# Order of the small matrix products of a hybrid diffusion step: alternating array halves, and column groups in whole visits

## The chip, the core and the metric

One core of a Trainium2 chip runs the whole kernel. The metric is the device time of one execution in microseconds, here the median of three runs. TensorE (PE) multiplies, VectorE (DVE), ScalarE (ACT) and GpSimd (POOL) do the elementwise work, and SyncE (SP) issues most of the DMAs. TensorE's array has 128 rows, along which a product sums, and 128 columns, its outputs. A product that needs only 64 rows or only 64 or 32 columns occupies a part of the array.

## The reference, cut

The reference takes 128 context tokens and 512 latent tokens of width 1024 through two layers. In each layer:

```
sh1, sc1, g1, sh2, sc2, g2 = split(silu(c) @ w_mod + b_mod, 6)          # adaLN, per stream
h = rmsnorm(x) * (1 + sc1) + sh1
z, xbc, dt, u, dq, dk, dv, wq, wk, wv = split(h @ w_in)
y_a = ssd_mixer(...)                     # Mamba-2 scan, both directions
y_b = s5_mixer(u, ...)                   # diagonal state space, both directions
y_c: s = q k^T / 8 for two halves (c = 0, 1) of each of 4 heads; softmax each
     (softmax_0 - lam * softmax_1) @ v   # differential attention
y_d: softmax([sink, q k^T / 8 + band mask]) @ v   # 8 query heads, 2 key heads, window 128
x = x + g1 * ((sum of gate_b * (y_b @ w_branch_b)) @ w_out)
x = x + g2 * (relu(rmsnorm(x)... @ w_fc1)^2 @ w_fc2)
```

Queries, keys and window values have 64 numbers a head, so the score products sum over 64 rows, and the window's product with the values has 64 outputs.

## The kernel before, in words

Activations lie feature-major in tiles of 128 features by 640 tokens, worked in halves of 320 tokens. Every large product (`mm3_step`, L221 to L223) is three products of high and low parts, on the whole array, 128 by 128. The weights are loaded by SP, rounded by ACT (L210) into the high part, and DVE or POOL makes the low part (L194).

Four kinds of small products use a part of the array only:

- `adaln` (L277), called by `adaln_ahead` (L304) for 36 pieces of 256 outputs: eight products, k = 0 to 7, each on 32 columns, at column group k mod 4 (L286). Their weights come through the ring `wa`, a quarter of the panel (two k) a DMA. Twelve more pieces, at the start, take theirs from `wm` tiles.
- `s5_build` (L476), eight blocks of four groups in each layer: for each group g, on column group g, four products of 112 columns (L646) and four of 16 (L650, L651), into the bank `pk`.
- `win_core` (L1241): for every token tile t (five) and key head n (two), pairs `hp` of query heads; a score tile `sc` of two banks holds the heads j = 0, 1 of the pair. The score products (L1264, L1266) sum over the 64 rows of key head n; masks are added by products with the identity (L1271); after the softmax and the transposes (L1301) head by head, the products with the values (L1306) write 64 columns, the half n of `po`.
- `diff_core` (L1376): for every token tile t and head h of a call, c = 0 and then c = 1: a score tile `sc` of two banks, filled by two products of 320 keys (L1394; one of 128 for t = 0, L1390) over the 64 rows of half c; then the maxima, the exponentials, the difference, transposes (L1423), the products with the values (L1428) and the square (L1430).

The tiles `sc`, `pt`, `raw` and adaLN's `acc` all come from `mx()`, a ring of two tiles of two PSUM banks.

The order of the work is static. A plan of letters (`PLAN`) advances generators, one step each, so that the chains of several mixers and the large products alternate; a scheduler then orders each engine's instructions ahead of time by priority (the place in the program) as their inputs come ready, and `tc.high_priority(offset=n)` moves what it encloses n places ahead. On the chip each engine takes its instructions in that order. Weights' preparation has `AHEAD = 2000`. In the steps named `b` (S5 matrices of layer 0) and in the MLP of layer 0 (its matrices for layer 1, and adaLN pieces) the small products go between large ones.

Of the kernel before, what the change touches and what calls it, by code (L numbers as in the profile page):

```python
# [39 lines left out]
AHEAD = 2000  # L40
NORM_POOL = (1, 4, 7)
NTAIL = 3
# buffers of the rings of tiles
# [3 lines left out]
# the engine of an elementwise step: v(ector) or p(ool)  # L47
# [4 lines left out]
# of the scan's blocks of latent chunks, those on the vector engine  # L52
SCAN = 5
# every so many low parts of operands is made on the pool engine
# [20 lines left out]
def hybrid_body(ctx: ExitStack, tc: tile.TileContext, a: dict, o: dict, dbg: dict):  # L75
# [21 lines left out]
    # ---------------------------------------------------------------- tiles  # L97
# [6 lines left out]
    def load_const(name, src, shape, into):  # L104
        """A constant, to be loaded behind the first loads, or later."""
        t = const(name, shape)
        into.append((t, src))
        return t
# [92 lines left out]
    def load_w(src, n=512, extra=False, ahead=AHEAD):  # L201
        """(high, low) of a weight tile; extra: in tiles of the phase's pool."""
# [22 lines left out]
    def mm3(ps, terms):  # L225
        """ps = sum over terms of stationary^T moving, each operand a (high, low) pair."""
# [3 lines left out]
    def split_w(w, kk):  # L230
        """Column block kk, of 128, of a panel."""
# [8 lines left out]
    def dense(src, act, evac):  # L240
        """One block of 128 outputs, feature-major: evac(half, psum [128, 320])."""
# [6 lines left out]
    def dense23(srcs, act, evacs):  # L248
        """Two or three blocks of 128 outputs, by halves of the tokens: a function of the half, yielding by block."""
# [12 lines left out]
    def streams(hf):  # L262
        """Token ranges of a half by stream: (stream, first, last) within the half."""
# [4 lines left out]
    # ------------------------------------------------------------- adaLN  # L268
# [8 lines left out]
    def adaln(l, parts, q, acc, out, raw):  # L277
        """mods[l][:, part*8 + 2q + (0, 1), stream] of one or two parts.

        acc: a bank of PSUM; out: 4 columns a part for the results; raw(part, n): quarter n of a panel of weights."""  # L280
        n = len(parts)
        for i, part in enumerate(parts):
            for k in range(KT):
# [4 lines left out]
                    start=(k < 4), stop=(k >= 4),  # L288
# [14 lines left out]
    def adaln_ahead(l, parts, after=()):  # L303
        """The pieces of the given parts, one a step."""  # L304
        for part in parts:
            for q in range(4):
# [9 lines left out]

                acc = mx()
                adaln(l, [part], q, acc[:, 0], acc[:, 1], raw)
# [4 lines left out]
    def step(gen, n=1):  # L323
        """The next n pieces of work that fills gaps."""
# [17 lines left out]
    # ---------------------------------------------------------------- norm  # L342
    def square_into(acc, x, k, hf):
        """acc += x[k]^2 on one half."""
# [8 lines left out]
    def norm_factor(acc, hf):  # L353
        """1/rms by token of one half, a quarter of it in each column; and the last instruction on the tensor engine."""
# [7 lines left out]
    def norm_spread(r, rb, hf):  # L362
        """The factor, on all partitions, into the half's bank of rb; the last instruction on the tensor engine."""
# [7 lines left out]
    def norm_mod(l, which, x, rb, hf, hh, hl):  # L371
        """(high, low) of rmsnorm(x)*g*(1+sc)+sh on one half, feature-major; rb: the norm's factor.

        A block of features a step."""
# [90 lines left out]
    # ------------------------------------------------------- S5 matrices  # L465
    s5m = {}

    def s5_build(l, where, after):
        """Per layer: the chunk matrices of the S5 mixer, into DRAM scratch; in steps, 4 groups each after the first.

        after(): an element of a tile before which no step need begin."""
# [23 lines left out]
        for w, shift in (("c", 0.25), ("s", 0.0)):  # L495
            # turns, less the nearest whole number of them
# [38 lines left out]
        # powers 1..8 of the transition of a chunk: re, -im, im  # L535
# [15 lines left out]
        # coef = (ab - 1) / lambda  # L551
# [19 lines left out]
        # exponents by position: input side, by 7-s (fwd 7-s, bwd s); output side (fwd t+1, bwd 8-t)  # L571
# [670 lines left out]
    def win_core(l, wv, qT, kT, var):  # L1242
# [4 lines left out]
        for t in range(NT):  # L1247
# [10 lines left out]
            for n in range(2):  # L1258
# [51 lines left out]
                if n == 0:  # L1310
                    yield
# [639 lines left out]
```

## Time and profile before

| | |
|---|---|
| median of 3 runs | 3173.34 us (3172.48 to 3176.21) |
| profiled execution | span 3172.2 us |
| PE busy | 3026.8 us, 95% |
| DVE busy | 1754.7 us, 55% |
| ACT busy | 1180.2 us, 37% |
| POOL busy | 956.7 us, 30% |

The profiled execution has no time beside its span; the span stands 1.1 us below the median. Busy is the union of an engine's instructions. A matrix product's record begins when it can enter and ends when its results are written, so that records in a row overlap: what a product costs is the distance of starts, not its duration. The profile's name of a shape, 64\*128 64x320, gives the array's rows and columns in use, and then the moving operand.

### The profile page before, as it was taken

To read this page: it belongs to the slowest core of one execution; us is meant where nothing else is said; L and a number is where in the kernel's file an instruction comes from. 1 tells how busy PE (TensorE), PEld (TensorE's weight loads), DVE (VectorE), ACT (ScalarE), POOL (GpSimd) and SP (SyncE) were. 2 spreads that over 40 slices of the span, in tenths; PEclk is the share of its full clock that TensorE was granted. 3 is DMA by queue.
4 is the path that set the end of the run, shared out by engine and by line. 5 is a ranking of instruction groups with operands and counts; after the bars stand their busy time and mean duration, and the time that the engine had idled before them with its cause. 6 is when DMAs were issued, how large, how long until landed. Compare 5 with 4: busy or idle time off the path is not lost. (4 is left out here: it accounts for less than half of the span.)

```text
span 3172.2 us, 54421 instructions
## 1 busy us (share of the span) xinstructions
PE 3026.8 (95%) x20846; PEld 2777.1 (88%) x20846; DVE 1754.7 (55%) x3866; ACT 1180.2 (37%) x2660; POOL 956.7 (30%) x1058
## 2 busy tenths in 40 slices
PE   8888898999999999999999889989999999999999
PEld 6878888898788889899988879878897899999999
DVE  6978836665532456376235686576674425533333
ACT  4234453243333242323234435423433333422323
POOL 1656505522210322144111670263131113211111
PEclk9999999999899999999999999989998999999999
DMA  7553243224331633444444323522251223222222
GB/s 280 173 171 99 77 134 106 78 94 128 123 98 47 213 114 131 142 145 156 136 147 136 127 78 103 149 86 62 80 188 56 71 90 126 64 75 76 74 77 84
DMA packets 240708, 364.23 MB, mean 115 GB/s; under 512 B 42144, under 2 KB 104352, under 8 KB 240448
## 3 DMA queue, kind: packets, MB, share of 16 engines
q1 hardware_dynamic: 225696, 336.97, 33.4%
q10 hardware_dynamic: 14752, 23.78, 2.1%
q8 instruction: 164, 2.69, 0.3%
q14 instruction: 96, 0.79, 0.1%
HBM read 294.98 MB, written 65.68 MB: 114 GB/s over the span
## 5 line engine op out<-in xcount | busy, mean ns | idle before, releaser
L194 POOL TENSOR_TENSOR wl<-wr,wh 128x512 fp32r<-128x512 f32 x207 | 282.3, 1364 | 1328.0 <-ACT wh L210 1059.2
L210 ACT CAST wh<-wr 128x512 fp32r<-128x512 f32 (+1 forms) x614 | 378.4, 620 | 623.5 <-PE dn L222 557.1
L194 DVE TENSOR_TENSOR wl<-wr,wh 128x512 fp32r<-128x512 f32 (+1 forms) x407 | 318.7, 786 | 326.2 <-ACT wh L210 311.3
L221 PE MATMUL dn<-hh,wh 128*128 128x320 f32 x1328 | 425.2, 320 | 7.2 <-ACT gah L1454 6.5
L223 PE MATMUL dn<-hh,wl 128*128 128x320 f32 x1328 | 423.6, 320 | 6.5 <-DVE wl L194 6.5
L222 PE MATMUL dn<-hl,wh 128*128 128x320 f32 x1328 | 423.2, 319 | 2.9 <-DVE hl L395 2.5
L221 PE MATMUL dn<-fh,wh 128*128 128x320 f32 x1008 | 315.3, 313 | 0.9 <-DVE x L1512 0.8
L221 PE MATMUL dn<-nh,wh 128*128 128x320 f32 x992 | 311.0, 314 | 1.6 <-DVE r L1718 1.6
L222 PE MATMUL dn<-fl,wh 128*128 128x320 f32 x1008 | 312.5, 310 | 0.0
L223 PE MATMUL dn<-fh,wl 128*128 128x320 f32 x1008 | 311.6, 309 | 0.0
L222 PE MATMUL dn<-nl,wh 128*128 128x320 f32 x992 | 308.7, 311 | 2.0 <-DVE nl L395 1.1
L223 PE MATMUL dn<-nh,wl 128*128 128x320 f32 x992 | 307.7, 310 | 0.0
L222 PE MATMUL dn<-wl,hh 128*128 128x256 f32 (+1 forms) x880 | 258.0, 294 | 17.5 <-DVE wl L194 15.0
L221 PEld LDWEIGHTS dn<-hh,wh 128*128 128x128 f32 x1328 | 257.1, 194 | 16.3 <-ACT gah L1454 7.0
L223 PEld LDWEIGHTS dn<-hh,wl 128*128 128x128 f32 x1328 | 256.7, 193 | 14.8 <-issue 7.3
L221 PE MATMUL dn<-wh,hh 128*128 128x256 f32 (+1 forms) x880 | 258.8, 296 | 7.1 <-ACT hsq L1174 3.7
L222 PEld LDWEIGHTS dn<-hl,wh 128*128 128x128 f32 x1328 | 256.9, 194 | 9.8 <-issue 4.5
L223 PE MATMUL dn<-wh,hl 128*128 128x256 f32 (+1 forms) x880 | 256.2, 292 | 0.0
L221 PE MATMUL dn<-B,wh 128*128 128x320 f32 x640 | 207.2, 325 | 9.3 <-ACT B L814 3.3
L1512 DVE SCALAR_TENSOR_TENSOR x<-dn,mod,x 128x192 f32<-128x192 f32 (+2 forms) x240 | 97.9, 436 | 206.3 <-PE dn L223 203.3
L222 PE MATMUL dn<-B,wh 128*128 128x320 f32 x640 | 202.2, 316 | 0.0
L223 PE MATMUL dn<-B,wl 128*128 128x320 f32 x640 | 200.9, 314 | 0.0
(410 smaller groups left out, 7066.1 us busy)
## 6 DMA issues: line engine op xcount, KB each, us to landing
wr<-in_w_fc_dram SPq DMA_DIRECT2D x256, 256.0 KB, 2.6
wa<-in_w_mod_dram SPq DMA_DIRECT2D x144, 256.0 KB, 3.4
wr<-in_w_gate_dram SPq DMA_DIRECT2D x128, 256.0 KB, 2.7
wr<-in_w_tok_dram SPq DMA_DIRECT2D x80, 256.0 KB, 2.9
wr<-in_w_branch_dram SPq DMA_DIRECT2D x64, 256.0 KB, 2.9
acc<-gth SPq DMA_DIRECT2D x48, 320.0 KB, 2.8
gold<-acc SPq DMA_DIRECT2D x48, 320.0 KB, 3.3
wm<-in_w_mod_dram SPq DMA_DIRECT2D x24, 512.0 KB, 8.8
```

Of the source, the lines that this page charges most:

```text
L194: engine.tensor_tensor(out=out, in0=full, in1=hi, op=ALU.subtract)
L210: nc.scalar.copy(out=hi, in_=raw)
L221: nc.tensor.matmul(ps, sh, vh, start=first, stop=False)
L222: nc.tensor.matmul(ps, sh, vl, start=False, stop=False)
L223: nc.tensor.matmul(ps, sl, vh, start=False, stop=last)
L1512: nc.vector.scalar_tensor_tensor(out=xs, in0=ps[:, c0:c1], scalar=mods[l][:, part * 8 + f, s:s + 1], in1=xs, op0=ALU.mult, op1=ALU.add)
```

## The change

- `VISIT = 600`, an offset of priority.
- `adaln` takes the list of its k. `adaln_ahead` asks for the piece's four weight tiles first, and then issues the products in a block of priority VISIT, k from 7 down to 0. The twelve pieces at the start are as before.
- `s5_build`: the loop over the four groups g becomes the innermost one, and the whole is a block of priority VISIT.
- `win_core`: instead of the pairs `hp` of one key head, an iteration takes query head g of both key heads n = 0, 1, bank n of `sc` each, and their score products alternate in n. Where the first key tile and the run behind it are neighbours (t = 1, 2), one product covers both. The masks follow. The products with the values wait for both heads' transposes and alternate in n. Both sets are blocks of priority VISIT.
- `diff_core`: both score tiles are taken at once, and the products alternate, c = 1, 0 for keys b = 0, then for b = 1, in a block of priority VISIT.

All else in the diff is the removal of comments. Its core:

```
+VISIT = 600
-    def adaln(l, parts, q, acc, out, raw):
+    def adaln(l, parts, q, acc, out, raw, ks=range(KT)):
-            for k in range(KT):
+            for n_, k in enumerate(ks):
-                    start=(k < 4), stop=(k >= 4),
+                    start=(n_ < 4), stop=(n_ >= 4),
...
+                for n in range(KT // 2):
+                    raw(part, n)
                 acc = mx()
-                adaln(l, [part], q, acc[:, 0], acc[:, 1], raw)
+                with tc.high_priority(offset=VISIT):
+                    adaln(l, [part], q, acc[:, 0], acc[:, 1], raw, range(KT)[::-1])
...
             pk = pb1()
-            for g in range(4):
-                rows = slice(32 * g, 32 * g + 32)
+            with tc.high_priority(offset=VISIT):
                 for c0, c1, z0, t0 in ((0, 112, 16, 1), (128, 240, 0, 0)):
-                    for ri in range(2):
+                    for ri in (1, 0):
+                        for g in range(4):
+                            nc.tensor.matmul(
+                                pk[32 * g:32 * g + 32, c0:c1], bz[:, ri, g, z0:z0 + 32],
+                                qt[:, ri, g, t0:t0 + 7].rearrange("p t m -> p (t m)"), start=(ri == 1), stop=(ri == 0),
+                            )
+                for ri, cc in ((0, craw[:, 0]), (1, ncr[:, 1])):
+                    for g in range(4):
                         nc.tensor.matmul(
+                            pk[32 * g:32 * g + 32, 112:128], bz[:, ri, g, 48:80], cc[:, g], start=(ri == 0),
+                            stop=(ri == 1),
                         )
...
+            rows = [slice(64 * n, 64 * n + 64) for n in range(2)]
+            whole_run = nk > 1 and run[0] == lone + 1
+            for g in range(4):
+                sc = mx()
+                with tc.high_priority(offset=VISIT):
+                    for k0, k1 in [(lone, run[1])] if whole_run else [(lone, lone + 1)] + [run] * (nk > 1):
+                        c0 = 0 if k0 == lone else 128
+                        for n in range(2):
                             nc.tensor.matmul(
+                                sc[:, n, c0:c0 + (k1 - k0) * 128], qT[rows[n], g, ct],
+                                kT[rows[n], k0:k1].rearrange("p k c -> p (k c)"), start=True,
+                                stop=not masks or k1 == lone + 1,
                             )
...
+                with tc.high_priority(offset=VISIT):
+                    for k in range(nk):
+                        for n in (1, 0):
                             nc.tensor.matmul(
+                                po[rows[n], g * 128:(g + 1) * 128], wv[:, idx[k], rows[n]], pT[n][:, k],
                                 start=(k == 0), stop=(k == nk - 1),
                             )
...
+                nb, w = (1, 128) if nk == 1 else (2, HF)
+                raw = [mx(), mx()]
+                with tc.high_priority(offset=VISIT):
+                    for b in range(nb):
+                        for c in (1, 0):
+                            gr = slice(64 * c, 64 * c + 64)
+                            keys = kT[gr, h, k0:k0 + nk].rearrange("p k c -> p (k c)")
+                            nc.tensor.matmul(
+                                raw[c][:, b, 0:w], qT[gr, h, ct], keys[:, b * w:(b + 1) * w], start=True, stop=True
+                            )
```

## Rows read from the trace of the kernel before

**Rows 1.** The page: busy time by engine, and PE in 40 slices.
```profile
PE 3026.8 (95%) x20846; PEld 2777.1 (88%) x20846; DVE 1754.7 (55%) x3866; ACT 1180.2 (37%) x2660; POOL 956.7 (30%) x1058
PE   8888898999999999999999889989999999999999
```

**Rows 2.** Busy time by stretch: PE, PEld, DVE, ACT, POOL; granted clock; DMA share, GB/s.
```profile
100.00:215.00 115.00, 99.77 (x870) 94.91 (x871) 104.91 (x195) 32.27 (x73) 82.12 (x84) 0.94 0.54 181
250.00:350.00 100.00, 85.29 (x510) 79.98 (x510) 96.81 (x193) 34.15 (x82) 76.64 (x123) 0.90 0.22 71
850.00:1010.00 160.00, 159.94 (x1045) 135.40 (x1044) 60.48 (x142) 59.31 (x143) 25.20 (x24) 1.00 0.26 84
1050.00:1700.00 650.00, 644.29 (x4707) 585.68 (x4705) 318.92 (x736) 198.19 (x408) 162.66 (x151) 1.00 0.45 147
2420.00:2580.00 160.00, 160.00 (x1045) 134.41 (x1044) 65.15 (x141) 58.62 (x143) 25.66 (x24) 1.00 0.23 77
```

**Rows 3.** Groups by line and form: shapes, count, busy us, mean ns, idle before.
```profile
L646 PE MATMUL pb<-s5qt,s5bz 128*32 128x112 f32 x512 | 58.3, 275 | 5.3 <-DVE s5qt L589 3.3 <-DVE s5bz L609 2.0
L286 PE MATMUL mx<-wa,cpad 128*32 128x256 f32 x576 | 63.3, 388 | 0.0
```

**Rows 4.** Timeline of PE at a differential score visit: start, us, line, tiles, shape, count.
```profile
655.31 0.27 PE L1423 MATMUL mx<-ident,dp 128*128 128x128 f32 x1
655.51 1.34 PE L1394 MATMUL mx<-d,BT 64*128 64x320 f32 x4
...
657.01 0.28 PE L223 MATMUL dn<-wh,hl 128*128 128x256 f32 x1
657.12 0.28 PE L221 MATMUL dn<-wh,hh 128*128 128x256 f32 x1
```

**Rows 5.** The same where two halves stand together; first the first two records alone.
```profile
1812.08 0.38 PE L1390 MATMUL mx<-d,dq 64*128 64x128 f32 x2
...
1812.08 0.49 PE L1390 MATMUL mx<-d,dq 64*128 64x128 f32 x4
1812.51 0.39 PE L221 MATMUL dn<-wh,hh 128*128 128x272 f32 x1
```

**Rows 6.** The same in the window attention: two heads' scores, then products with values.
```profile
897.55 0.49 PE L1264 MATMUL mx<-wkT,xs 64*128 64x128 f32 x2
897.87 0.81 PE L1266 MATMUL mx<-wkT,xs 64*128 64x384 f32 x2
898.83 0.48 PE L1264 MATMUL mx<-wkT,xs 64*128 64x128 f32 x2
899.89 1.09 PE L1306 MATMUL pb<-wp,wv 128*64 128x128 f32 x8
```

**Rows 7.** The same at an S5 block: its first products, and the next large ones.
```profile
1367.93 0.95 PE L646 MATMUL pb<-s5qt,s5bz 128*32 128x112 f32 x8
...
1371.17 0.21 PE L651 MATMUL pb<-s5nc,s5bz 128*32 128x16 f32 x2
1371.32 0.42 PE L221 MATMUL dn<-fh,wh 128*128 128x320 f32 x1
```

**Rows 8.** The same at adaLN: a visit of four records, and a whole piece.
```profile
1066.67 0.63 PE L286 MATMUL mx<-wa,cpad 128*32 128x256 f32 x4
1067.23 0.42 PE L221 MATMUL dn<-mh,wh 128*128 128x320 f32 x1
...
1237.25 1.07 PE L286 MATMUL mx<-wa,cpad 128*32 128x256 f32 x16
1238.25 0.42 PE L221 MATMUL dn<-fh,wh 128*128 128x320 f32 x1
```

**Rows 9.** Busy time of L1306 alone by stretch: PE and count, PEld, clock, DMA.
```profile
850.00:1010.00 160.00, 25.23 (x182) 19.19 (x182) 1.00 0.26 84
2420.00:2580.00 160.00, 27.83 (x200) 21.07 (x200) 1.00 0.23 77
```

**Rows 10.** What TensorE's idle time before L1394 ended with.
```profile
  ACT mx L1430: 2.1, 5
```

More of the change, by code (lines that the diff above doesn't have):

```diff
@@ L1257, in win_core @@
             po = pb1()
-            for n in range(2):
-                gr = slice(64 * n, 64 * n + 64)
-                for hp in range(2):
-                    sc = mx()
-                    for j in range(2):
-                        q = qT[gr, 2 * hp + j, ct]
-                        nc.tensor.matmul(sc[:, j, 0:128], q, kT[gr, lone], start=True, stop=True)
-                        if nk > 1:
+            rows = [slice(64 * n, 64 * n + 64) for n in range(2)]
+            whole_run = nk > 1 and run[0] == lone + 1
@@ L1266, in win_core @@
+            for g in range(4):
[4 more added lines that the diff above has]
+                        for n in range(2):
                             nc.tensor.matmul(
-                                sc[:, j, 128:nk * 128], q, kT[gr, run[0]:run[1]].rearrange("p k c -> p (k c)"),
-                                start=True, stop=not masks,
-                            )
@@ L1270, in win_core @@
-                            for i, (pos, mk) in enumerate(masks):
-                                nc.tensor.matmul(
-                                    sc[:, j, (1 + pos) * 128:(2 + pos) * 128], identb, maskb[:, mk],
-                                    start=False, stop=(i == len(masks) - 1),
-                                )
-                    scv = sc[:, :, :nk * 128]
-                    m = tmp([128, 2], "wm")
-                    nc.vector.tensor_reduce(out=m, in_=scv, axis=AX.X, op=ALU.max)
@@ new lines, in win_core @@
+                                sc[:, n, c0:c0 + (k1 - k0) * 128], qT[rows[n], g, ct],
+                                kT[rows[n], k0:k1].rearrange("p k c -> p (k c)"), start=True,
+                                stop=not masks or k1 == lone + 1,
+                            )
+                    for n in range(2):
+                        for i, (pos, mk) in enumerate(masks):
+                            nc.tensor.matmul(
+                                sc[:, n, (1 + pos) * 128:(2 + pos) * 128], identb, maskb[:, mk],
+                                start=False, stop=(i == len(masks) - 1),
+                            )
@@ new lines, in win_core @@
+                scv = sc[:, :, :nk * 128]
+                m = tmp([128, 2], "wm")
+                nc.vector.tensor_reduce(out=m, in_=scv, axis=AX.X, op=ALU.max)
+                sk = sink[:, g::4]
+                nc.vector.scalar_tensor_tensor(out=m, in0=m, scalar=0.125, in1=sk, op0=ALU.mult, op1=ALU.max)
+                nm_ = tmp([128, 2], "wnm")
+                nc.vector.tensor_scalar(out=nm_, in0=m, scalar1=-1.0, scalar2=None, op0=ALU.mult)
+                p = [tw([128, 512], "wp") for _ in range(2)]
@@ new lines, in win_core @@
+                sm = tmp([128, 2], "wsm")
+                for n in range(2):
+                    nc.scalar.activation(
+                        out=p[n][:, :nk * 128], in_=scv[:, n], func=AF.Exp, bias=nm_[:, n:n + 1], scale=0.125,
+                        accum_out=sm[:, n:n + 1],
+                    )
+                es = tmp([128, 2], "wes")
+                nc.vector.tensor_tensor(out=es, in0=sk, in1=m, op=ALU.subtract)
+                nc.scalar.activation(out=es, in_=es, func=AF.Exp)
+                nc.vector.tensor_tensor(out=sm, in0=sm, in1=es, op=ALU.add)
@@ new lines, in win_core @@
+                rc = tmp([128, 2], "wrc")
+                nc.vector.reciprocal(out=rc, in_=sm)
+                pt = mx()
+                pT = []
+                for n in range(2):
+                    pn = p[n][:, :nk * 128]
+                    nc.vector.tensor_scalar(out=pn, in0=pn, scalar1=rc[:, n:n + 1], scalar2=None, op0=ALU.mult)
+                    for k in range(nk):
+                        kc = slice(k * 128, (k + 1) * 128)
+                        nc.tensor.transpose(pt[:, n, kc], p[n][:, kc], ident)
+                    pT.append(pn.rearrange("p (k c) -> p k c", c=128))
+                    nc.scalar.copy(out=pT[n], in_=pt[:, n, :nk * 128].rearrange("p (k c) -> p k c", c=128))
@@ L1308, in win_core @@
+                with tc.high_priority(offset=VISIT):
+                    for k in range(nk):
+                        for n in (1, 0):
+                            nc.tensor.matmul(
+                                po[rows[n], g * 128:(g + 1) * 128], wv[:, idx[k], rows[n]], pT[n][:, k],
                                 start=(k == 0), stop=(k == nk - 1),
                             )
-                if n == 0:
+                if g == 1:
                     yield
@@ L1383, in diff_core @@
                 scs, ms = [], tmp([128, 2], "dm")
-                for c in range(2):
-                    gr = slice(64 * c, 64 * c + 64)
-                    sc = mx()
-                    keys = kT[gr, h, k0:k0 + nk].rearrange("p k c -> p (k c)")
-                    q = qT[gr, h, ct]
-                    if nk == 1:
-                        nc.tensor.matmul(sc[:, 0, 0:128], q, keys, start=True, stop=True)
-                        sv = sc[:, 0:1, 0:128]
-                    else:
-                        for b in range(2):
-                            nc.tensor.matmul(sc[:, b, 0:HF], q, keys[:, b * HF:(b + 1) * HF], start=True, stop=True)
-                        sv = sc[:, :, 0:HF]
+                nb, w = (1, 128) if nk == 1 else (2, HF)
[5 more added lines that the diff above has]
+                            keys = kT[gr, h, k0:k0 + nk].rearrange("p k c -> p (k c)")
+                            nc.tensor.matmul(
+                                raw[c][:, b, 0:w], qT[gr, h, ct], keys[:, b * w:(b + 1) * w], start=True, stop=True
+                            )
+                for c in range(2):
+                    sv = raw[c][:, 0:nb, 0:w]
                     nc.vector.tensor_reduce(out=ms[:, c:c + 1], in_=sv, axis=AX.XY, op=ALU.max)
```

33 lines of the change are left out of this document (removed).

## The prediction

> **What bounds the kernel now.** I read the page first: PE is busy for 3026.8 of 3172.2 us, in no slice under 80%, and no other engine over 55% [rows 1]. That average has two kinds of stretch, so the table by stretch comes second [rows 2]. In the second half of the window attention of either layer (850 to 1010 and 2420 to 2580 us) and in the MLP of layer 0 (1050 to 1700 us) PE is busy 99 to 100% and DVE at most half: there a microsecond off PE is a microsecond off the kernel. In 100 to 215 and 250 to 350 us DVE is busy 91 and 97% and PE 87 and 85%: there DVE's chain sets the end, and the granted clock of 0.94 and 0.90 shows that TensorE spends a part of the time at 1.2 instead of 2.4 GHz, because it waits. The groups by line come third [rows 3]. Every product that the code writes stands in the trace as two records: `s5_build` issues 16 products of 112 columns a block, 16 blocks, and L646 has 512 records [rows 3]. So all counts below are records.
>
> **What a small product costs now.** The timeline shows two prices, one of streaming and one of the way in and out.
>
> Eight records of 112 columns, all on one column group, last 0.95 us, and one of them 0.28 in the mean [rows 3, 7]: the starts lie (0.95 - 0.28) / 7 = 0.096 us apart, 0.86 ns a column. By that 128 columns stream in 0.11 us, 256 in 0.22, 320 in 0.27.
>
> A differential score visit is four records of 320 columns, one half c of the array's rows [rows 4]. From the transpose's start at 655.31 to the second large product behind it at 657.01 pass 1.70 us; less the transpose of 128 columns, 0.11, and a large product, 0.11 by the next one's start, some 1.47 us are the visit's. Streaming is 4 x 0.27 = 1.07 of them, so the records follow one another. The other 0.40 us are the way in and out: the array runs empty, the new weights load in the open, and the same back.
>
> Do two halves run at once, if their records are neighbours? In thirteen places of the trace the scores of t = 0 stand in visits of two or four. In a visit of four [rows 5] the first two records together last 0.38 us, one alone 0.37; the four take 0.42 to the next large product's start, where four that follow one another (L1264, same 128 columns) would take four times 0.11 and the way in. So halves of rows run at once, and the loads of the second round are hidden. For columns, adaLN shows the same with four groups: 16 records of 256 columns in a visit of 1.07 us [rows 8], which is four rounds of 0.21, not sixteen.
>
> **The change part by part**, in PE time.
>
> *Differential scores.* 64 visits of four now (32 head tiles with t > 0, two halves each; 256 records). After: 32 visits of eight records in four rounds, 1.07 + 0.40. That removes 32 x 1.47 = 47 us. The scores of t = 0, thirteen visits of two or four into eight of four, give some 3 more. Sum 50.
>
> *Window scores.* Two heads' scores stand at 897.55 and 898.83, 1.28 us apart with the masks [rows 6]; 64 such visits have t > 0. After, 32 pairs: both key heads run at once, and one way in and out falls away. Streaming of a visit is 0.85 us where there are 512 keys and 0.64 where 384, 0.75 in the mean, and the way some 0.35: 1.1 us x 32 = 35, and 2 for t = 0. The number of mask products stays. Sum 37.
>
> *Products with the values.* 480 records of 128 columns, eight of them 1.09 us [rows 6], so 0.11 apart, in 80 visits. After: 240 rounds, 40 visits; 240 x 0.11 = 26, and 40 ways in and out at some 0.3 = 12. Sum 38. If the loads of the two column halves did not hide behind the other's products, a round would take up to twice as long and 12 were left; adaLN's column groups hide theirs [rows 8], so I take 38.
>
> *S5 matrices.* A block takes from 1367.93 to 1371.32, 3.39 us [rows 7]: 32 records at 0.096 and 16 short ones at 0.03. With the four groups side by side 8 rounds of 0.096 and 4 of 0.03 stay, 0.9 us. 2.45 x 16 = 39 us, half of it in layer 0 (100 to 215 us), half in the MLP.
>
> *adaLN.* The groups already run at once; what goes is the cutting up. The 576 records from `wa` lie in 85 visits, from that at 1066.67 on, of 2 to 26 records each. From the first start of a visit of four to the next large product pass 0.56 us, of a whole piece 1.00 [rows 8]; with the emptying before and the load after, half of the 0.40 found in rows 4, 0.76 and 1.20. A visit of four is 0.63 busy, so 0.13 of each visit is not in the busy time: 63.3 [rows 3] + 85 x 0.13 = 74 us now, 36 x 1.20 = 43 after. Sum 31. In exchange the first product (k = 7) waits for the last of four weight tiles, 256 KB each. The DMA engines are busy 45% there [rows 2], so I cost it at nothing; it is covered by the large products that the scheduler can place before the visit, and would cost up to a DMA's landing of 3.4 us where it can't.
>
> All parts: 50 + 37 + 38 + 39 + 31 = 195 us of PE time, 2977 us if all of it counted.
>
> **What of it counts.** In the three full stretches: adaLN's 31, half of S5's, 19.5, and of the window's 75 the share of its records that lie there, (182 + 200) of 480 [rows 9], 80%: 60. That is 110 us on the path. Outside lie 85: the differential scores (50), S5 of layer 0 (19.5), the first window tiles (15). The S5 blocks of layer 0 and some of the differential steps lie where DVE is busy over 90% and PE already waits, and there the gain becomes a longer wait for DVE; others lie among large products that fill PE. I take half, 43, between none and all. A longer wait lowers the clock more often: I take 5 us, for in the stretches named the clock already costs TensorE up to a tenth. 110 + 43 - 5 = 148. 3173.3 - 148 = 3025 us.
>
> What could be late next: in the full stretches nothing near, DVE at 38 to 49%. The exponentials of a step need both halves' maxima before and after, so that taking both `mx` tiles at once adds no wait which the step did not have: c = 1 waited for the same tile, and TensorE's idle time by it is 2.1 us in all [rows 10].
>
> **Rivals.**
>
> *The other engines' chains keep their times.* All of the 85 outside the full stretches turns into waits, and the clock, at 1.2 GHz for longer, takes 15 to 20 more: 3173 - 110 + 18 = 3081. For it: DVE at 97% of 250 to 350. Against it: most differential steps lie in 350 to 500 and 600 to 800, where PE has large products. 0.20.
>
> *Slower: visits block the queue.* PE takes its instructions in order, and a visit now begins with the operand that comes last: the second `mx` tile, the fourth weight tile, the second head's transposes. There are 32 + 8 differential, 40 window score, 40 value, 36 adaLN visits, 156 in all, and everything behind such a visit, the large products too, stands still while it waits. At 148 / 156 = 0.95 us each the gain is gone; at 1.5 us each the time is 3173 + 156 x 0.55 = 3259. For it: an offset of 600 places a visit ahead of its cover, if the scheduler's times are too short. Against it: now such a wait is 0.4 us, five times [rows 10]. 0.04.
>
> *The records are not taken side by side.* If the scheduler still parts the visits, or halves wait for one another, only ways in and out that fall away count: 32 x 0.4 + 32 x 0.35 + 40 x 0.3 = 36, and half of adaLN's, 15: 3122. Against it: rows 5 and 8. 0.04.
>
> *Passes in strict order.* If the two records of a product had to start in the program's order, only the second of one could run beside the first of the next: five rounds instead of four for a head tile's differential scores (32 x 0.27 = 9 us), one more for every window visit (32 x 0.3 and 40 x 0.11, 14 us), and S5's 32 records in 17 rounds of 0.096 instead of 8 (16 x 0.86, 14 us). Of these 37 us about 25 lie on the path: 3050. Against it: the four records of rows 5 stand in two rounds, not three, and adaLN's sixteen in four. 0.04. The Trainium skill states such a rule, "TensorE: Matmul & The Clock Gate", Part 3, The mechanism: matrix products start and end strictly first in, first out. No row speaks against it for whole products; by the two records of one the trace differs.
>
> **How the numbers follow.** The forecast, 3025 with half of the outside part, has 0.68; the others as given. It alone reaches from 2977 (all 195) to some 3068 (110 and nothing of the rest, less 5). The range goes over into the first rival, to 3085, for it holds 0.2; low 2980. A difference under 0.2%, 6 us, cannot be told from none. Faster by more: the forecast and all rivals but the second, and a little less for an order of the instructions that turns out worse elsewhere, 0.94; within 0.2%: 0.02; slower 0.04.
>
> **What would show it.** In the changed profile: L1394 in 32 visits of eight records, each some 1.1 to 1.3 us; L646 and its kin in a visit of 0.9 to 1.1 us a block; L286 from `wa` in some 36 visits of sixteen; PE's busy time lower by 150 to 190 us; PE still 99% busy in the MLP, and the MLP of layer 0 shorter by some 50 us, the one of layer 1 unchanged. Where DVE was over 90% busy, the stretch should stay as long and PE's idle time grow. Wrong would be: pairs of records that start 0.1 us or more apart; PE idle in front of L1394, L286 or L1306 by over 0.5 us each; or large products late in stretches that this change does not touch.

## The result and the profile after

The changed kernel takes 3076.4 us (median of four runs, 3075.0 to 3080.9), the kernel before beside it 3174.8 us: a ratio of 0.9688, 95% interval 0.9666 to 0.9710. That is 98 us less, where 148 were forecast. The profiled execution spans 3073.2 us.

The page of the changed kernel, against [rows 1]: PE's busy time is 135 us lower, its share of the span almost the same; the other engines do what they did.

```profile
PE 2892.0 (94%) x20782; PEld 2691.9 (88%) x20782; DVE 1759.4 (57%) x3866; ACT 1175.9 (38%) x2660; POOL 952.9 (31%) x1058
PE   8778898999899999999999889989999999999999
```

Where did the 98 us come from? I cut the trace by events that every version has: the first sum of a norm, the last differential score of a layer (L1394, now L1407), the last window product with values (L1306, now L1321). The table holds the distances between these starts in us; the rows of the single edits and of the later runs belong to the sections below. The distances are read from one profiled execution each.

| kernel | before it | to the last diff score, layer 0 | window | to the norm | MLP 0 | to the last diff score, layer 1 | window | to the norm | MLP 1 | span |
|---|---|---|---|---|---|---|---|---|---|---|
| before | 17.4 | 767.9 | 235.5 | 113.1 | 562.0 | 654.8 | 219.5 | 128.8 | 473.2 | 3172.2 |
| changed | 18.1 | 777.6 | 192.4 | 110.3 | 540.9 | 656.3 | 191.9 | 114.5 | 471.1 | 3073.2 |
| only_window | 17.9 | 772.2 | 196.7 | 118.9 | 561.7 | 657.3 | 194.8 | 114.5 | 471.7 | 3105.7 |
| only_adaln | 17.9 | 770.4 | 234.9 | 104.4 | 555.6 | 651.4 | 220.1 | 128.8 | 471.7 | 3155.3 |
| only_s5 | 18.5 | 774.1 | 233.0 | 113.1 | 550.8 | 657.8 | 213.8 | 128.8 | 473.2 | 3163.1 |
| no_diff | 19.1 | 772.9 | 194.5 | 110.3 | 540.2 | 655.3 | 193.5 | 114.5 | 473.2 | 3073.6 |
| no_offset | 17.7 | 774.0 | 200.3 | 103.0 | 610.2 | 654.6 | 186.9 | 119.9 | 473.1 | 3139.7 |
| offset_adaln | 17.9 | 774.1 | 202.7 | 103.0 | 553.9 | 654.0 | 186.9 | 119.9 | 473.1 | 3085.4 |
| by_keys | 18.6 | 779.1 | 196.2 | 103.2 | 543.9 | 654.9 | 195.3 | 114.2 | 470.7 | 3076.1 |
| light_chains | 18.5 | 756.6 | 207.2 | 103.2 | 541.5 | 634.4 | 194.1 | 114.0 | 471.2 | 3040.8 |
| light_by_keys | 18.0 | 694.2 | 235.1 | 102.9 | 541.0 | 588.8 | 219.7 | 121.4 | 471.6 | 2992.7 |
| own_max | 18.5 | 745.2 | 208.9 | 103.3 | 542.7 | 615.4 | 188.7 | 130.8 | 473.2 | 3026.7 |

The two windows and what follows them give 88 us, the MLP of layer 0 gives 21. The two longest stretches, from the start of a layer to its last differential score, give nothing: they are 10 and 1.5 us longer. The MLP of layer 1, which the change does not touch, stays.

The same stretches in the table by stretch (busy time of PE, PEld, DVE, ACT, POOL; granted clock; DMA share, GB/s), first of before: the window and MLP of layer 0; then of the changed kernel: the stretch that [rows 2] begins with, the window, the MLP.

```profile
785.30:1020.80 235.50, 230.13 (x1425) 191.29 (x1423) 100.94 (x262) 86.88 (x230) 41.89 (x40) 0.95 0.30 97
1133.90:1695.90 562.00, 556.29 (x4114) 514.06 (x4113) 282.88 (x656) 174.36 (x359) 146.59 (x137) 1.00 0.42 137
```

```profile
100.00:215.00 115.00, 85.38 (x877) 79.58 (x878) 109.61 (x196) 32.98 (x75) 82.14 (x84) 0.84 0.57 184
795.70:988.10 192.40, 177.38 (x1316) 153.10 (x1316) 99.67 (x259) 82.84 (x224) 35.47 (x35) 0.96 0.34 107
1098.40:1639.30 540.90, 529.47 (x4115) 498.90 (x4114) 288.85 (x656) 171.19 (x359) 147.10 (x137) 0.99 0.44 143
```

In 100 to 215 us PE is busy 85.4 instead of 99.8 us [rows 2] and the granted clock falls from 0.94 to 0.84: the S5 blocks of layer 0 became short there, and the time turned into a longer wait for DVE, now busy 109.6 of 115. In the MLP PE's busy time fell by 27 us, but its idle time doubled, from 5.7 to 11.4.

**The new visits.** The groups by line and form (shape, count, busy us, mean ns, idle before), against [rows 3]:

```profile
L652 PE MATMUL pb<-s5qt,s5bz 128*32 128x112 f32 x512 | 19.7, 287 | 7.7 <-DVE s5bt L594 5.1 <-DVE s5qt L594 2.6
L287 PE MATMUL mx<-wa,cpad 128*32 128x256 f32 x576 | 43.2, 385 | 2.6 <-DMA wa<-in_w_mod_dram 2.6
L1321 PE MATMUL pb<-wp,wv 128*64 128x128 f32 x480 | 35.5, 283 | 2.8 <-ACT wp L1317 2.8
```

And PE's timeline at one visit of each kind, with the next large product behind it: the scores of two heads and their masks, the products with values, an S5 block, an adaLN piece.

```profile
871.29 1.13 PE L1277 MATMUL mx<-wkT,xs 64*128 64x512 f32 x4
872.35 0.40 PE L1284 MATMUL mx<-maskb,identb 128*128 128x128 bf16 x4
...
987.52 0.88 PE L1321 MATMUL pb<-wp,wv 128*64 128x128 f32 x12
988.33 0.42 PE L223 MATMUL dn<-hl,wh 128*128 128x320 f32 x1
...
1321.17 0.97 PE L652 MATMUL pb<-s5qt,s5bz 128*32 128x112 f32 x32
1321.96 0.23 PE L658 MATMUL pb<-s5c,s5bz 128*32 128x16 f32 x8
1322.02 0.23 PE L658 MATMUL pb<-s5nc,s5bz 128*32 128x16 f32 x8
1322.18 0.41 PE L223 MATMUL dn<-nl,wh 128*128 128x320 f32 x1
...
1103.73 1.07 PE L287 MATMUL mx<-wa,cpad 128*32 128x256 f32 x16
```

All four stand in rounds. Thirty-two records of an S5 block take 0.97 us where eight took 0.95 [rows 7]. Four records of 512 columns take 1.13 us: two rounds of 0.44 by the 0.86 ns a column, and the end of the last.

The differential scores are another matter. PE, DVE and ACT at one head tile (t > 0) of the changed kernel, its scores, maxima and exponentials:

```profile
660.29 1.34 PE L1407 MATMUL mx<-d,BT 64*128 64x320 f32 x4
661.67 0.82 DVE L1412 TENSOR_REDUCE dm<-mx 128x1 f32<-128x640 f32 x1 [2.58 <-PE mx L1407]
666.02 1.34 PE L1407 MATMUL mx<-d,BT 64*128 64x320 f32 x4
667.85 0.82 DVE L1412 TENSOR_REDUCE dm<-mx 128x1 f32<-128x640 f32 x1
668.70 0.17 DVE L1415 TENSOR_SCALAR dnm<-dm 128x2 f32<-128x2 f32 x1
668.96 0.80 ACT L1425 ACTIVATE dp<-mx,dnm 128x640 f32<-128x640 f32 x1 [2.71 <-DVE dnm L1415]
669.65 0.19 ACT L1425 ACTIVATION_READ_ACCUMULATOR dp<-mx,dnm 128x1 f32 x1
669.75 0.78 ACT L1425 ACTIVATE dp<-mx,dnm 128x640 f32<-128x640 f32 x1
670.42 0.20 ACT L1425 ACTIVATION_READ_ACCUMULATOR dp<-mx,dnm 128x1 f32 x1
```

The two halves do not meet: four records at 660.29, the other four 5.7 us later, each visit still 1.34 us [rows 4]. The program's order alternates them, but each half has a tile of the ring `mx` to itself, and the order on TensorE, made ahead of time, lets each go by itself. The run by_keys, below, tests whether the two tiles are the reason. Of 77 visits 67 have four records and 10 have two; all 64 visits of the tiles with t > 0 hold four records of 320 columns.

### The profile page after: what moved, and what is told of

Read it like the earlier page. It is cut to its first block, busy times and chain, and to the rows that moved or that the text cites. A ratio compares the mean times of both kernels' runs of the same rounds, so it can differ in the third digit from the quotient of the medians.

```text
span 3073.2 us, 54263 instructions
## 1 busy us (share of the span) xinstructions
PE 2892.0 (94%) x20782; PEld 2691.9 (88%) x20782; DVE 1759.4 (57%) x3866; ACT 1175.9 (38%) x2660; POOL 952.9 (31%) x1058
## 5 line engine op out<-in xcount | busy, mean ns | idle before, releaser
L223 PE MATMUL dn<-wl,hh 128*128 128x256 f32 (+1 forms) x880 | 258.9, 295 | 20.2 <-DVE wl L195 17.4
L222 PE MATMUL dn<-B,wh 128*128 128x320 f32 x640 | 205.3, 322 | 11.5 <-ACT B L824 3.6
L224 PE MATMUL dn<-B,wl 128*128 128x320 f32 x640 | 200.3, 313 | 0.0
```

Source lines behind the costliest of these rows:

```text
L222: nc.tensor.matmul(ps, sh, vh, start=first, stop=False)
L223: nc.tensor.matmul(ps, sh, vl, start=False, stop=False)
L224: nc.tensor.matmul(ps, sl, vh, start=False, stop=last)
```

## The experiments

**Each part alone.** Four kernels take the kernel before and one of the changed functions.

```
only_window: before, with win_core of the changed kernel
only_adaln:  before, with adaln and adaln_ahead of the changed kernel
only_s5:     before, with s5_build of the changed kernel
only_diff:   before, with diff_core of the changed kernel
```

> The kernel before with the window attention of the changed kernel alone (scores and products with the values alternate between the key heads). Theory A (the window part is most of the gain, the differential part none): from the end of the differential steps to the norm behind the mixers the changed kernel is 46 and 42 us shorter in its two layers, of which adaLN has a few in layer 0 and none in layer 1, so 3174 - 80 to 85, 3090 to 3094 us. Rival B (each part gives what was predicted and the parts take it back from each other): 3174 - 68 = 3106 us.

Measured: 3106.8 us, ratio 0.9777 (0.9755 to 0.9799), 71 us less. The term of the sum was 67.

> The kernel before with the adaLN pieces in whole visits alone. Predicted 31 us. Theory A: the trace of the changed kernel has 42 visits instead of 85 and a wait of 2.4 us before one of them, so 12 to 20 us, 3154 to 3162. Rival B: 31 us, 3143.

Measured: 3164.7 us, 0.9964 (0.9950 to 0.9979), 11 us less, 3 above the range of theory A. The MLP of layer 0 became 6.4 us shorter, the stretch before it 8.7. TensorE's time for the pieces themselves fell by 24 us (from 74.5 to 50.2 us, start to next start and 0.2 us a visit for the way in and out). But the S5 blocks, which keep their old order here, fell into 30 visits instead of 17 and took 5 us more, and PE's waits between 1050 and 1700 us rose from 5.6 to 11.5 us.

> The kernel before with the S5 blocks' products round the four column groups alone. Theory A: nothing in layer 0, where DVE's chain sets the end, and 7 to 8 whole blocks of 2.4 us in layer 1: 14 to 20 us, 3154 to 3160, and the end of the steps that build layer 0's matrices not earlier than before by over 3 us. Rival B: half of layer 0's 20 as well, 3145.

Measured: 3163.1 us, 0.9956 (0.9941 to 0.9971), 14 us less, 3 above the range of theory A: 11 in the MLP of layer 0, nothing ahead of it. What held PE up behind the S5 blocks (waits of PE, 1370 to 1500 us of only_s5: total, times, longest):

```profile
PE dn L222 <- DVE r L1724: 4.6, 3, 2.7
```

`r` belongs to the MLP's own chain (DVE's step between the two large products); in this stretch DVE is busy 104 of 130 us, with the S5 operations among the rest. So the large products now run into DVE.

> The kernel before with the differential scores of the changed kernel alone (both tiles asked for at once, products alternate). Theory A: the two halves of a head tile still stand in visits of their own, some 9 us apart, because each needs one tile of the ring and goes as soon as that one is free: no gain, 3174 within 10, and 64 or more visits of four records. Rival B: pairs in 32 visits, 20 to 47 us, 3127 to 3154.

Measured: 3177.2 us, 1.0000 (0.9987 to 1.0014). 77 visits, as in the changed kernel.

The four add up to 96 us, the change has 98. The intervals leave each of these some 5 to 7 us, so no interaction of the parts can be seen beyond that.

**The changed kernel without its differential part.**

```
no_diff: the changed kernel, with diff_core of before
```

> The changed kernel with the differential part undone. Theory A: the same time, 3076 within 6. Rival G (that part costs, for each half is one visit and both tiles are asked for at once): 3060 to 3070.

Measured: 3079.2 us, 0.9688 (0.9669 to 0.9706), the same ratio as the change. With only_diff this says from both sides that the edit gives no time here.

**Halves that do meet.** Here one score tile holds both halves for one block of keys, so that the two products that are to run together need the same tile.

```
-                raw = [mx(), mx()]
+                raw = []
+                for b in range(nb):
+                    raw.append(mx())
...
-                                raw[c][:, b, 0:w], qT[gr, h, ct], keys[:, b * w:(b + 1) * w], start=True, stop=True
+                                raw[b][:, c, 0:w], qT[gr, h, ct], keys[:, b * w:(b + 1) * w], start=True, stop=True
```

> The changed kernel with the differential scores grouped the other way: a score tile holds both halves c for one block of 320 keys, one bank each, so that the two products of a pair need one tile and one visit; the maxima and the sums of the two tiles are joined by two more small DVE operations and two more exponentials a step (0.2 us each). Theory A (pairs were parted only because each half waited for a tile of its own): 64 visits of four records in two rounds, 0.94 us instead of 1.47, 34 us of TensorE time less; a fourth to a half of it counts where DVE and the chains set the end in part: 3076 - 9 to 17, so 3059 to 3067. Rival C (in the mixers' stretches TensorE's time is not the bound at all): 3076 within 6, the visits are 0.94 us all the same. Rival D (halves of rows do not run side by side for 320 keys): visits stay at 1.47 us and the time goes up by the added operations, 3076 to 3090.

Measured: 3075.1 us, 0.9667 (0.9646 to 0.9689): the same time as the change. All 72 visits have four records in pairs. PE's timeline of by_keys at one of them:

```profile
676.31 0.81 PE L1406 MATMUL mx<-d,BT 64*128 64x320 f32 x4
677.05 0.39 PE L222 MATMUL dn<-wh,hh 128*128 128x256 f32 x1
```

0.81 us, and 0.74 to the next large product, instead of 1.34 and 1.28. From the first start of a visit to the next other record the visits take 58.2 us in all, against 92.2: 34 us of TensorE's time are saved, and none of it counts. The stretch by_keys was meant for, first the changed kernel, then by_keys:

```profile
215.00:795.70 580.70, 535.74 (x3584) 490.10 (x3582) 376.56 (x766) 245.31 (x557) 231.11 (x282) 0.93 0.35 106
```

```profile
215.00:797.70 582.70, 524.85 (x3628) 484.53 (x3627) 384.20 (x802) 253.36 (x622) 232.59 (x286) 0.94 0.37 108
```

PE's busy time is 11 us lower, and the stretch 2 us longer. Here less work for TensorE does not shorten the stretch.

**What sets it: VectorE's work, or the tiles?** Two kernels shorten the chain of the steps without an edit to TensorE's products. Both leave out five of the convolution's seven taps and the maxima of the differential scores; light_chains does so in the changed kernel, light_by_keys in by_keys.

```
-            for k in range(1, 7):
+            for k in range(1, 2):
...
-                    nc.vector.tensor_reduce(out=ms[:, c:c + 1], in_=sv, axis=AX.XY, op=ALU.max)
...
-                        out=pv, in_=scs[c], func=AF.Exp, bias=nms[:, c:c + 1], scale=0.125, accum_out=sm[:, c:c + 1]
+                        out=pv, in_=scs[c], func=AF.Exp, bias=zb, scale=0.001, accum_out=sm[:, c:c + 1]
```

> The changed kernel without five of the convolution's seven taps and without the maxima of the differential scores (the exponentials take a fixed bias and a smaller scale): TensorE's work is untouched, VectorE has some 60 x 0.89 us of taps and some 72 maxima of up to 0.82 us less, about 110 us in both layers, nearly all of it in the stretches from the start of a layer's projections to its last differential scores (777.6 and 656.3 us in the changed kernel). If the chains of the other engines set the end of these stretches, they become shorter by 30 to 100 us in all and the time falls to 2975 to 3046. If TensorE's time sets it, VectorE's work lies beside it and the time stays at 3076 within 6 us.

Measured: 3047.1 us, 0.9598 (0.9570 to 0.9626), 29 us below the change and 1 us above the range that the chains' theory gave: DVE has 118 us less to do (1640.9 of busy time), and a quarter of it shows.

> The same left out, on the kernel whose score tile holds both halves for one block of keys, where TensorE has 33 us less to do (a run with a third less of score visits gained nothing with the chains at full length). If the shorter chains still set the end, this comes out as the run without those taps and maxima does, within 6 us. If TensorE becomes the bound once the chains are shorter, it is lower by 10 to 33 us. If TensorE was the bound all along, lower by 33 as well, but then the run of by_keys with full chains should have been lower too.

Measured: 2995.1 us, 0.9433 (0.9403 to 0.9463): 52 us below light_chains, more than the 34 that TensorE's visits could give, and so none of the three outcomes. The layout gains nothing with the maxima and 52 us without them. What the maxima do in by_keys is to tie the tiles together: both exponentials of either tile wait for the maximum over both. So I measured in the traces how long the two score tiles of a head tile are held, from the first score's start in a tile to the end of the last exponential that reads it, added over both and averaged over the 32 head tiles with t > 0. For the head tile above it is (670.62 - 660.29) + (669.84 - 666.02), 14.2 us.

| kernel | tiles held, us a head tile | first score to first transpose, us | span |
|---|---|---|---|
| before | 18.8 | 19.3 | 3172.2 |
| changed | 20.9 | 20.7 | 3073.2 |
| no_diff | 18.8 | 19.3 | 3073.6 |
| by_keys | 22.8 | 22.4 | 3076.1 |
| light_chains | 15.5 | 18.8 | 3040.8 |
| light_by_keys | 4.8 | 13.5 | 2992.7 |
| own_max | 10.3 | 18.7 | 3026.7 |

By_keys pairs the products and yet holds its tiles 1.9 us longer. From the changed kernel on, the spans stand in the order of the time that the tiles are held, but for no_diff, which holds its tiles 2.1 us less than the changed kernel and takes the same time. The column beside it is the mean length of a step, from its first score to its first transpose; the spans stand in its order as well, with the same exception. So the two explanations have to be told apart. The tiles suggested the next run.

**Tiles set free earlier, with all of the computation.** In own_max, made from by_keys, the exponential takes the maximum of its own block of keys; `ef`, the exponential of a block's own maximum less the common one, brings both blocks to one scale afterwards, through the sums `sb` and the factors `rb`.

```
+                for b in range(nb):
+                    nc.vector.tensor_scalar(out=nmb[:, b], in0=mb[:, b], scalar1=-0.125, scalar2=None, op0=ALU.mult)
                     for c in range(2):
                         nc.scalar.activation(
                             out=full[c][:, b * w:(b + 1) * w], in_=raw[b][:, c, 0:w], func=AF.Exp,
-                            bias=nms[:, c:c + 1], scale=0.125, accum_out=sb[:, b, c:c + 1],
+                            bias=nmb[:, b, c:c + 1], scale=0.125, accum_out=sb[:, b, c:c + 1],
...
+                    nc.scalar.activation(out=ef, in_=ef, func=AF.Exp)
+                    nc.vector.tensor_tensor(out=sb, in0=sb, in1=ef, op=ALU.mult)
...
+                        rb = ef[:, b]
+                        nc.vector.tensor_tensor(out=rb, in0=rb, in1=rc, op=ALU.mult)
```

> by_keys with an exponential that takes the maximum of its own block of keys, the two blocks being brought to one scale afterwards by small factors: a score tile is then read out and free as soon as its own two products and its own maximum are done, without waiting for the other tile. TensorE's work is that of by_keys; VectorE has some 0.8 us a head tile more (six more small operations of about 0.17 us, some of them in place of others), about 27 us in all, and ScalarE 32 small exponentials. If what sets the differential steps is how long the two score tiles stay occupied by each other's maximum (leaving the maxima out made by_keys 52 us shorter than the same with the tiles by halves), the time falls well below by_keys' 3075, to 3010 to 3060. If it is VectorE's operations themselves, or the length of the chain of one step, it is 3075 to 3100.

Measured: 3032.8 us (3028.4 to 3034.1), 0.9559 (0.9543 to 0.9575): 41 us below the change by the ratios, and faster than both kernels of this case. DVE does more (1797.5 us busy, 38 more than in the changed kernel), TensorE's work is that of by_keys. So neither the sum of DVE's operations nor TensorE's work (by_keys) sets the end of these stretches. How long the score tiles are held fits; it is not shown apart from the length of a step, which the expectation put with the other outcome and which this edit shortens as well, from 22.4 us in by_keys to 18.7. For the tiles speaks light_chains: its step is as long (18.8), DVE has 157 us less to do there than in own_max, and yet it is 14 us slower by the spans, with its tiles held 5 us longer. No run gives the ring a third tile, which would test it alone. One head tile of own_max, the same lines as above:

```profile
665.59 0.81 PE L1406 MATMUL mx<-d,BT 64*128 64x320 f32 x4
666.84 0.82 DVE L1409 TENSOR_REDUCE dm<-mx 128x2 f32<-128x640 f32 x1
667.69 0.17 DVE L1414 TENSOR_SCALAR dnm<-dm 128x2 f32<-128x2 f32 x1
668.15 0.53 ACT L1416 ACTIVATE dp<-mx,dnm 128x320 f32<-128x320 f32 x1
...
669.08 0.20 ACT L1416 ACTIVATION_READ_ACCUMULATOR dp<-mx,dnm 128x1 f32 x1
671.50 0.81 PE L1406 MATMUL mx<-d,BT 64*128 64x320 f32 x4
```

The first tile is read out at 669.28, 2.2 us before the second one's scores begin. In the changed kernel above, the first tile had its maximum at 662.5, and no tile was read before 668.96, after the maximum of the second. The two stretches up to the last differential score are 73 us shorter than in the changed kernel; some 27 of them come back behind these, where the window of layer 0 and the stretch to the norm of layer 1 are 16 us longer each. What stays open is how much of the 41 us is the tiles' freedom, how much the shorter step and how much TensorE's shorter visits, which may count once the tiles do not bind.

**The offset.** First no offset at all, then adaLN's alone.

```
no_offset:    -VISIT = 600
              +VISIT = 0
offset_adaln: offset=0 in s5_build, win_core and diff_core
```

> The changed kernel with VISIT = 0: the same products in the same program order, without the priority of the visits. Theory A: running side by side needs neighbours in the queue, and the scheduler parts them without the offset: the window products lose a part of their 71 us, adaLN all of its 11: 3095 to 3125, with more visits. Rival E (the order of the loops alone does it): 3076 within 8, the same number of visits.

Measured: 3140.9 us, 0.9882 (0.9864 to 0.9900), 16 us above the range of theory A. The adaLN pieces from `wa` fall into 149 visits, 108 of them of one product (two records), where the changed kernel has 43; L287 from `wa` is busy 100.9 us instead of 43.2, and the MLP of layer 0 takes 610 us. The order k from 7 down without the offset is worse than the order of before (562 us). Window and S5 visits stay whole.

> The changed kernel with the offset of 600 on adaLN's pieces alone, 0 on the other three kinds. Without any offset only adaLN's visits fell apart (162 instead of 55) and the MLP of layer 0 became 69 us longer, while window and S5 visits stayed whole. If adaLN alone needs the offset: 3067 to 3080, the stretches around the window of layer 1 and the one behind the window of layer 0 up to 7 us shorter, the MLP of layer 0 at 541 within 6. If the S5 blocks need it too, the MLP of layer 0 is longer by 10 us or more: above 3083.

Measured: 3086.2 us, 0.9718 (0.9689 to 0.9747), above the bound that was set: the MLP of layer 0 is 13 us longer, with S5's first products cut into 20 small visits (7 in the changed kernel) beside 14 whole ones. That is some 6 us of TensorE's time, start to next start and 0.2 us a visit. The adaLN pieces, which keep their offset, also lie in 49 visits instead of 43, some 4 us. So S5 without its offset costs time where adaLN has one, in part through adaLN; the run does not part the two further. The gains expected around the windows came (7 us behind the window of layer 0, 5 in that of layer 1), but the window of layer 0 and the stretch behind that of layer 1 lost 10 and 5.

**Products with values, head by head.** The loop over n goes outside that over k.

```
-                    for k in range(nk):
-                        for n in (1, 0):
+                    for n in (1, 0):
+                        for k in range(nk):
```

> The changed kernel with the window's products with the values issued key head by key head inside the same visit (n outer, k inner). What runs side by side is undone there, the 40 visits are kept. Theory A: 480 records at 0.11 us in a row instead of 240 rounds, 26 us of TensorE time more, of which 80 to 100% counts: 3097 to 3102. Rival F (the gain comes from fewer visits alone, 40 ways in and out): 3076 within 5.

Measured: 3087.5 us, 0.9713 (0.9694 to 0.9731), some 8 us above the change by the ratios, a third of what was expected and neither of the two outcomes. The intervals of the two ratios just overlap, so the 8 us alone would not show a difference. TensorE's own time for these visits does: 48.7 us from start to next start instead of 36.4, in the same 40 visits. A visit in values_by_head:

```profile
840.71 1.14 PE L1321 MATMUL pb<-wp,wv 128*64 128x128 f32 x12 [0.57 <-ACT wp L1317]
```

One after the other, twelve records would take eleven distances of 0.11 and the last one's 0.27, 1.5 us; paired they take 0.88. At 1.14 about half of the pairing is still there, though six records of one half of the columns stand ahead of six of the other.

## Why the prediction was right, and where it was not

The time lies in the stated range, but 51 us above the forecast of 3025 and 5 below the first rival's 3081; the range holds it because it was drawn over that rival. Of the 195 us of PE time in the sum 135 came off. Of the signs named, the S5 block's visit (1.0 us) and the longer wait for DVE came; the 32 visits of eight for the differential scores, 150 to 190 us less of PE's busy time, PE 99% busy in the MLP (it is 98%) and an MLP of layer 0 shorter by 50 us did not.

By the single runs the missing 50 us are these: the differential scores 25 short of what was counted, adaLN 20 (31 counted, 11 measured), S5 15 (29 counted, 14 measured), the window 4 better. 25 + 20 + 15 - 4 = 56; the sum had taken off 5 for the clock, which the single runs contain: 51.

**Right: what a visit costs.** Streaming, the way in and out, and rounds of neighbours were read from single visits, and they hold. With 0.2 us a visit for the emptying ahead of it and the load behind, half of the prediction's 0.40, adaLN's pieces from `wa` took 57.5 + 85 x 0.2 = 74.5 us before (74 in the sum) and take 40.1 + 43 x 0.2 = 48.7 now (43 in the sum): there are 43 visits, not 36. Counted the same way, the S5 blocks took 65.4 and take 26.1 in only_s5, where all 16 are whole, 39 us less, as in the sum; in the changed kernel, with one block cut up, they take 31.6. The window's scores went from 70.8 to 36.2 us and the products with values from 74.2 to 36.4, start to next start: 72 of the 75 us.

So the rival *the records are not taken side by side* falls for three of the four kinds. *Passes in strict order* falls too: four records of 512 columns in three rounds would take 2 x 0.44 and the last one's 0.64, 1.52 us, and in two rounds 1.08; they take 1.13. The rule of the Trainium skill beside that rival ("TensorE: Matmul & The Clock Gate", Part 3, The mechanism) is not contradicted for whole products here; by the number of rounds of the records, this visit differs from it.

**Right: where it counts fully.** In the window stretches TensorE was the bound, and only_window gave 71 us for the term of 67.

**Wrong: the differential scores.** Two steps failed. The text had 32 visits of eight, because "c = 1 waited for the same tile": it took the small price of one wait [rows 10] for proof that both tiles come free together. That wait was one of the order as it stood. In the new order the halves stand 5.7 us apart in the head tile shown, without a wait for a tile; with one tile for both, all 72 visits are pairs. And "I take half" was wrong for this part: by_keys has 34 of the 50 us and gains nothing. The large products in 350 to 500 and 600 to 800 us were the argument against that rival; they are there, but less work for TensorE did not end the stretch sooner. That the steps wait for one another's tiles is the explanation that fits own_max, with the open end named there.

**Wrong: S5 of layer 0.** The 10 us counted are nothing. The text had named the reason itself, DVE over 90% busy [rows 2], and its sign appeared: the stretch as long as before, PE's idle time up by 14 us.

**Mis-sized: the MLP of layer 0**, 21 us shorter instead of some 50. First, not all of adaLN lies there: 57 of its 85 visits did, with 28 of the 36 pieces, 52.5 us by the same count, so that 28 x 1.20 leaves 19 of its 31 us; 17 came. Secondly, PE's idle time went from 5.7 to 11.4 us. "In the full stretches nothing near" rested on DVE's mean of half; behind an S5 block DVE comes last, for up to 2.7 us in only_s5. Thirdly, one S5 block, the first of layer 1, is still cut up, into 15 visits between 1250 and 1278 us, and takes some 6.7 us instead of 1.2 (the first of them in PE's timeline of the changed kernel):

```profile
1250.01 0.38 PE L652 MATMUL pb<-s5qt,s5bz 128*32 128x112 f32 x2
1257.55 0.39 PE L652 MATMUL pb<-s5qt,s5bz 128*32 128x112 f32 x6
1261.58 0.57 PE L652 MATMUL pb<-s5qt,s5bz 128*32 128x112 f32 x10
```

**Right: visits that block the queue cost little.** PE waits for the last weight tile three times (waits of PE in the MLP of layer 0: total, times, longest), 2.6 us in all, where 0.95 us for each of 156 visits would have eaten the gain.

```profile
PE mx L287 <- DMA wa<-in_w_mod_dram: 2.6, 3, 2.2
```

The rival *the other engines' chains keep their times*, at 3081, comes within 5 us, but in part by luck. Of the 85 us outside the full stretches only S5's 20 became a wait. The differential scores' 50 never left TensorE (their visits take 90.3 us before and 92.2 now), and the first window tiles' 15 counted, since the window gave all of its term. Against that, adaLN and S5 gave less in the full stretches than its 110. Its 18 us for the clock stand by themselves in no run; the granted clock is 0.970 before and 0.962 now in the mean. What it leant on, DVE's share of 97%, was not the cause in the differential steps: 118 us less of DVE's work gave 29, and own_max has 38 us more of it and is 41 faster.

## What to carry over

Price a small product by its visit: the columns it streams, once a round, and a way in and out of some 0.4 us. Then ask what each stretch waits for before adding the savings up. Products that are to run side by side should write the same PSUM tile, so that one release sets both free: here that made pairs of all visits, though it gave no time by itself. And where no engine is full and less work for the fullest one gives nothing, measure how long the few tiles are held, from the first write to the last read: no share of busy time shows it.

## What was not expected of the hardware

- Products of two column halves overlap even when they don't alternate: 12 records, six of one half and then six of the other, took 1.14 us, between 0.88 (alternating) and 1.5 (by the distances, one after the other).
- Four weight loads of a visit on one half of the rows are spread over 0.83 us, those of a visit on both halves over 0.30 (PEld at 660.29 of the changed kernel and at 665.59 of own_max):

```profile
660.29 0.83 PEld L1407 LDWEIGHTS mx<-d,BT 64*128 64x128 f32 x4 [0.16 <-issue]
```

```profile
665.59 0.30 PEld L1406 LDWEIGHTS mx<-d,BT 64*128 64x128 f32 x4 [0.16 <-issue]
```
